# A one-layer decoder step on one core: norm factors spread by matmuls, a different start, and another queue order in the last products

## The chip, the cores and the metric

The kernel runs on one core of one Trainium2 chip. The time is the device time of one execution in microseconds (us). Five engines run their own instruction queues side by side: TensorE (PE in the rows, PEld for its weight loads), VectorE (DVE), ScalarE (ACT), GpSimd (POOL) and SyncE (SP), which issues most DMA transfers. An instruction waits at the head of its queue until what it needs is there, and all behind it wait too.

## The reference

One step over T = 576 tokens: 512 of a new sequence and 8 x 8 of running ones, model width D = 1024. All is float32.

```python
def _rmsnorm(x, g):
    y = x * lax.rsqrt(jnp.mean(x * x, axis=-1, keepdims=True) + EPS)
    return y * g

def _swiglu(h, w_up, w_down):                    # D_FF = 2816
    a, g = jnp.split(h @ w_up, 2, axis=-1)
    return (jax.nn.silu(g) * a) @ w_down

x = x + 0.5 * _swiglu(_rmsnorm(x, g_ffn1), w_ffn1_up, w_ffn1_down)
x = x + mixer(_rmsnorm(x, g_mix))                # GLA and mLSTM, 4 heads each, gated and merged
x = x + 0.5 * _swiglu(_rmsnorm(x, g_ffn2), w_ffn2_up, w_ffn2_down)
y = _rmsnorm(x, g_final)
# in the mLSTM, for t >= s:   Dm = exp(b_t - b_s + i_s - m_t), else 0;   s = (q k^T) * Dm
```

The outputs are y and the new states of both mixers.

## The kernel before, in words

Everything is stored transposed: a tile x[k] holds 128 of the 1024 channels by 576 tokens, so there are KT = 8 tiles of x, and a product accumulates over 8 channel tiles in PSUM. For accuracy each operand is split into a high and a low part (`hi` by a copy on ScalarE, `lo` = source minus `hi` on VectorE), and a product is three matmuls per channel tile and half of the tokens (HALF = 288): weight-hi by x-hi, weight-hi by x-lo, weight-lo by x-hi (`mm3`, line 121). A dense product of all channels is 8 x 3 x 2 = 48 matmuls of 288 columns (`dense`).

**Norms.** The gain is folded into the split of x (`split_x`); the factor 1/rms of a token is applied behind the product. `Norm.square` squares x[k] on ScalarE and adds the squares up on GpSimd. `Norm.start` sums them over the channels with matmuls against ones, packed in four groups of 32 partitions (`packed_sum`, line 155), then takes the root (ScalarE) and the reciprocal (VectorE, line 225). `Norm.finish` calls `unpack` (line 161): four `partition_broadcast` on GpSimd spread the packed row over all partitions into the tile r.

**The feed-forward parts (`ffn`).** Of the 22 slices f of D_FF the first two (PLAIN) are two dense products each (gate, then linear part). All others go by seven quarter-size products (a Strassen-like scheme, blocks A11, S2, A12, S3, S1, A22, S4), for which `Norm.combine` forms sums of quarters of x on VectorE and ScalarE, and `sums` forms sums of weight quarters on VectorE and GpSimd. After every group of 4 slices come 8 blocks `d` of the down product, which add into x[o]. From the third slice on the order is written by hand (`manual_schedule`): `run(i, work)` issues the matmuls of a block, then what was put off to this tick (`posts`, filled by `later(ticks, fn)`), then the block's events: weight loads (`load_up`, `load_down`), and `prep` of the block 4 ahead (`hi` on ScalarE, `lo` on VectorE). `seven` puts off the steps behind the seven products; its first one copies the result of A11 on ScalarE (tile s), and A12 adds into that same PSUM bank. When a `d` block is done, `done` adds it to x[o] on VectorE, and in the last group calls `after(o)`.

In the second feed-forward part the last 8 down products run twice, once for each half of the tokens (`parts=((0,), (1,))`), 12 matmuls each. There `after` squares x[o] for the final norm, scales x[0] and x[4] by g_final on ScalarE, and behind the third block of the second half calls `finish(ends[0])`: broadcasts, 8 products with r (k = 0 and 4 on GpSimd, the other six on VectorE) and 8 output DMAs, alternating between SP and ScalarE. The same follows for the second half at the end.

**The start.** The weights of the first two products and the 8 tiles of x are loaded; ScalarE and VectorE split them; the gate product of slice 0 runs through all 8 tiles, then the linear product, then the gate product of slice 1 (`ahead=1`), with the raw results copied out of PSUM since r is not there yet.

**Outside the hand-written order** a planner places instructions by its own cost estimates and the order of the program: the start, the first two slices, both mixers, and the final part.

**The mLSTM (`mlstm`).** For each of 4 heads GpSimd broadcasts two rows (Mb, ib, lines 963 and 964), VectorE forms Dd = min(Mb + tok, 0) in four 128x128 instructions (line 62), ScalarE takes the exponential, GpSimd multiplies by the triangular mask `tri`, and VectorE multiplies by q k^T to St; the same for the short sequences with Ds and `tri8`. Line numbers 53, 56, 62 and 65 are helpers (`tt`, `stt`, `ts`, `act`); go by the tiles.

Of the kernel before, what the change touches and what calls it, by code (L numbers as in the profile page):

```python
# [36 lines left out]
def step_kernel(ctx: ExitStack, tc: tile.TileContext, a):  # L37
# [125 lines left out]
    class Norm:  # L163
# [25 lines left out]
        def add(self, k):  # L189
            self.split(k)  # L190
            self.square(k)

        def combine(self, q, pool):
# [39 lines left out]
    def ffn(x, norm, wup, wdn, fp, after, ahead=0, parts=((0, 1),)):  # L233

# [1 line left out]

        r = early = None

        def up(f, i):
            ps = dense(wup[f, :, i], norm.parts, KT)
            if f >= ahead:
                return ps
            t = fp.tile([P, T], F32, name="raw", tag="mh3", bufs=2)
            act(halves(t), ps, AF.Copy)
            return halves(t)

        def new_mid(i):
            return [fp.tile([P, T], F32R, name=f"m{n}", tag=f"m{n}{i}", bufs=2) for n in "hl"]

        mids = [[]]
        for f in range(PLAIN):
            if f == 0 and not ahead:
                midway.append(norm.start)
            pg = early or up(f, 0)
            early = None
            if f == 0:  # L260
                for q in range(4):
                    norm.combine(q, fp)
            pa = up(f, 1)
            if f == 0:
                if ahead:
                    midway.append(norm.start)
                    early = up(1, 0)
                r = norm.finish()
# [35 lines left out]
        def prep(i):  # L304

            b = blocks[i]
            if i % 2 == 0:
                pair[0] = [wp.tile([P, KT, P], F32R, name=f"w{n}", tag=f"w{n}", bufs=3) for n in ("hi", "lo")]
            if b[0] == "d":
                n = size[b[1]]  # L310
                src = raw["d"][b[1:]]
            else:
                n = 4
                src = raw[b[0]][b[1]]
            hi, lo = (t[:, 4 * (i % 2):4 * (i % 2) + n, :] for t in pair[0])
            act(hi, src, AF.Copy)
            tt(lo, src, hi, ALU.subtract)
            parts_of[i] = hi, lo

# [37 lines left out]
        for i, b in enumerate(blocks):  # L357
            if b[0] == "d" and b[2] % 2 == 0:
                on(i - 8, load_down, i)
            on(i - 4, prep, i)  # L360

        def later(d, fn):
            posts.setdefault(tick[0] + d, []).append(fn)
# [25 lines left out]
        def run(i, work):  # L389

            for m in work:
                nc.tensor.matmul(m[0], lhsT=m[1], rhs=m[2], start=m[3], stop=m[4], skip_group_check=m[5])  # L392
            for fn in posts.pop(tick[0], ()):
                fn()
            for fn, a_ in events.pop(i, ()):
                fn(*a_)
            tick[0] += 1

        with tc.manual_schedule():
# [4 lines left out]
            for i, b in enumerate(blocks):  # L404
                if b[0] == "d":
                    _, g, o, hfs = b
                    n = size[g]
                    hi, lo = parts_of.pop(i)
                    ps = pd.tile([P, 2, 512], F32, name="pd", tag="pd")
                    work = [(ps[:, hf, :HALF], wt[:, k, :], xt[:, hf * HALF:(hf + 1) * HALF],  # L410
                             k == 0 and m == 0, k == n - 1 and m == 2, False)
                            for k in range(n) for m, (wt, xt) in enumerate(
                                ((hi, mids[g][k][0]), (hi, mids[g][k][1]), (lo, mids[g][k][0]))) for hf in hfs]
                    half = 12 if len(work) > 12 else len(work)
                    run(i, work[:half])
# [12 lines left out]
                f, n = b  # L428
# [30 lines left out]
    with pool("f1") as fp:  # L459
        x = [fp.tile([P, T], F32, name=f"x{k}") for k in range(KT)]  # L460
        n1 = Norm(x, g_ffn1, fp)

        def load(*ks):
# [4 lines left out]
        ready.append(split_w(a["wup1"][0, :, 0], KT, 2, lambda: load(0, 1)))  # L468
        load(2, 3)
        ready.append(split_w(a["wup1"][0, :, 1], KT))  # L470
        load(4, 5, 6, 7)
        nc.sync.dma_start(out=cst, in_=a["cst"])
        for k in range(KT):
            n1.square(k)
# [6 lines left out]
        ffn(x, n1, a["wup1"], a["wdn1"], fp, after, ahead=1)  # L481
        midway.append(n2.start)
        first = [win_tile(), win_tile()]
        r = n2.finish()
# [3 lines left out]
    with pool("mx") as mp:  # L488
# [416 lines left out]
        with pool("ml") as gp:  # L905
# [7 lines left out]
            def mlstm(h):  # L913
# [110 lines left out]
                ts(by16(Ds), padded(Mb), tok[:, 0, NC, h:h + 1], ALU.add, 0.0, ALU.min)  # L1024
                act(Ds, Ds, AF.Exp)
                tt(Ds, Ds, tri8, ALU.mult, eng=nc.gpsimd)
# [75 lines left out]
    with pool("f2") as fp:  # L1102
        n4 = Norm(x, None, fp)
        ends = (slice(0, HALF), slice(HALF, T))

        def finish(s):
            r = n4.finish()
            for k in range(KT):
                if k % 4 == 0:
                    tt(x[k][:, s], x[k][:, s], r, ALU.mult, eng=nc.gpsimd)  # L1110
                else:
                    stt(x[k][:, s], x[k][:, s], g_fin[:, k:k + 1], ALU.mult, r, ALU.mult)
                (nc.scalar if k % 2 else nc.sync).dma_start(out=a["yT"][:, k, s], in_=x[k][:, s])

        def after(o, part):
            n4.square(o, ends[part[0]])
            if o % 4 == 0:
                act(x[o][:, ends[part[0]]], x[o][:, ends[part[0]]], AF.Copy, scale=g_fin[:, o:o + 1])
            if part == (1,) and o == 0:
                midway.append(lambda: n4.start(ends[0]))  # L1120
            if part == (1,) and o == 2:
                finish(ends[0])

        ffn(x, n3, a["wup2"], a["wdn2"], fp, after, parts=((0,), (1,)))
        n4.start(ends[1])
        finish(ends[1])

def _lay(i):  # L1130
# [45 lines left out]
    for j in range(4):  # L1176
# [17 lines left out]
    cst = [s == t_, U, tri8, np.ones((P, P)), (np.isin(s % 32 // 8, (0, 2)) & (np.arange(NB) < 1)[None, :]),  # L1194
           s // 32 == np.arange(4)[None, :], np.full((P, 1), EPS),
           *(np.broadcast_to(s == 32 * g, (P, P)) for g in range(4))]
    out["cst"] = np.concatenate([np.asarray(v, np.float32) for v in cst], 1)
# [50 lines left out]
```

## Time and profile before

| | before |
|---|---|
| median of 3 runs | 1648.14 us (1646.6 to 1650.25) |
| the profiled execution | 1647.72 us |
| its span in the profile | 1645.9 us |
| TensorE busy | 1574.6 us, 96% |
| VectorE busy | 1092.0 us, 66% |
| ScalarE busy | 668.4 us, 41% |
| GpSimd busy | 331.7 us, 20% |
| mean granted TensorE clock | 0.989 |

The profiled execution took 1.8 us more than its span, which lies around it, and is 0.4 us below the median. A timeline row reads: start, duration, engine, line, operation, out<-in, count of merged instructions, and in brackets how long the engine had been idle and who ended that.

### The profile page before, as it was taken

What the parts mean: (1) busy time and instruction counts of PE and PEld (TensorE: products, weight loads), DVE (VectorE), ACT (ScalarE), POOL (GpSimd) and SP (SyncE); (2) the same over time, 40 slices, a digit from 0 to 9 for tenths busy, and PEclk for the clock granted to TensorE, in tenths of its full rate; (3) what the DMA queues carried; (4) which work ended last, traced back from release to release, by engine and by line L of the source; (5) the groups of instructions that cost most, each with busy time, mean ns of one, the idle gap of its engine ahead of it and who ended that gap; (6) DMA issues with size and microseconds to landing.
All of it is one profiled execution on the core that took longest, in us unless ns stands there. A gap on an engine that the chain in (4) does not pass through costs nothing.

```text
span 1645.9 us, 29867 instructions
## 1 busy us (share of the span) xinstructions
PE 1574.6 (96%) x12332; PEld 1528.1 (93%) x12332; DVE 1092.0 (66%) x1808; ACT 668.4 (41%) x1104; POOL 331.7 (20%) x333
## 2 busy tenths in 40 slices
PE   6899999999999999999999999999999999999982
PEld 5899999999989989999998989999989999999982
DVE  7797777776597667653555757633578877777752
ACT  6343333434644342531334344521454343343441
POOL 3343223221200000000111011003223422323212
PEclk9999999999999999999999999999999999999996
DMA  5232232223522313323432434442222233233231
GB/s 176 71 96 91 78 104 89 80 88 101 183 78 93 108 61 99 105 92 118 132 120 87 140 109 147 154 148 78 81 81 78 96 98 96 77 99 94 65 90 58
DMA packets 58752, 166.23 MB, mean 101 GB/s; under 512 B 6008, under 2 KB 12920, under 8 KB 57592
## 3 DMA queue, kind: packets, MB, share of 16 engines
q1 hardware_dynamic: 57464, 163.14, 30.7%
q8 instruction: 97, 1.59, 0.4%
q10 hardware_dynamic: 1152, 1.18, 0.2%
q14 instruction: 39, 0.32, 0.1%
HBM read 142.89 MB, written 21.38 MB: 100 GB/s over the span
## 4 chain that ended last, share of the span: by engine, by line
PE 85%; DVE 6%; issue 3%; ACT 3%; POOL 2%; DMA 1%; POOLq 1%; SPq 0%; ACTq 0%; DVEq 0%
PE pd L121 34%; PE pd L392 31%; PE pm L392 11%; PE pm L780 2%; DVE wlo L53 1%; PE pm L506 1%; ACT whi L65 1%; PE pm L718 1%; PE pm L1002 1%; DVE xl L56 1%; PE pm L646 1%; DVE xtl L53 1%; DVE xt L56 1%; PE pm L1055 1%; PE pm L1000 0%
## 5 line engine op out<-in xcount | busy, mean ns | idle before, releaser
L65 ACT ACTIVATE whi<-wst 128x512 fp32r<-128x512 f32 (+2 forms) x298 | 217.5, 742 | 438.5 <-PE pd L121 263.9
L53 DVE TENSOR_TENSOR wlo<-wst,whi 128x512 fp32r<-128x512 f32 (+2 forms) x298 | 267.2, 898 | 34.1 <-ACT whi L65 25.5
L121 PE MATMUL pd<-xh,whi 128*128 128x288 f32 x1168 | 259.1, 300 | 15.8 <-ACT xh L65 7.4
L121 PE MATMUL pd<-xl,whi 128*128 128x288 f32 x1168 | 254.1, 297 | 4.1 <-DVE xl L56 4.1
L121 PE MATMUL pd<-xh,wlo 128*128 128x288 f32 x1168 | 253.8, 297 | 0.8 <-DVE wlo L53 0.8
L121 PEld LDWEIGHTS pd<-xh,whi 128*128 128x128 f32 x1168 | 189.1, 189 | 22.0 <-ACT xh L65 7.4
L121 PEld LDWEIGHTS pd<-xl,whi 128*128 128x128 f32 x1168 | 188.8, 189 | 7.3 <-DVE xl L56 6.0
L121 PEld LDWEIGHTS pd<-xh,wlo 128*128 128x128 f32 x1168 | 188.7, 189 | 4.1 <-issue 3.0
L53 POOL TENSOR_TENSOR t<-t,r 128x288 f32<-128x288 f32 (+1 forms) x80 | 102.6, 1283 | 419.8 <-DVE t L53 408.1
L392 PE MATMUL pd<-mh,whi 128*128 128x288 f32 x704 | 157.3, 297 | 18.2 <-DVE x L56 18.0
L56 DVE SCALAR_TENSOR_TENSOR x<-pd,x 128x576 f32<-128x576 f32 (+1 forms) x112 | 79.6, 711 | 133.6 <-PE pd L392 107.5
L392 PE MATMUL pd<-ml,whi 128*128 128x288 f32 x704 | 156.4, 296 | 0.0
L392 PE MATMUL pd<-mh,wlo 128*128 128x288 f32 x704 | 156.2, 296 | 0.0
L392 PE MATMUL pd<-xh,whi 128*128 128x288 f32 x480 | 143.1, 298 | 5.6 <-ACT s L65 4.2
L65 ACT ACTIVATE whi<-S 128x512 fp32r<-128x512 f32 x160 | 98.9, 627 | 120.6 <-PE pd L392 69.5
L392 PE MATMUL pd<-xh,wlo 128*128 128x288 f32 x480 | 142.3, 296 | 0.0
L392 PE MATMUL pd<-xl,whi 128*128 128x288 f32 x480 | 142.1, 296 | 0.0
L392 PE MATMUL pm<-xth,wlo 128*128 128x288 f32 x480 | 141.5, 295 | 0.0
L392 PE MATMUL pm<-xtl,whi 128*128 128x288 f32 x480 | 141.5, 295 | 0.0
L392 PE MATMUL pm<-xth,whi 128*128 128x288 f32 x480 | 141.5, 295 | 0.0
L392 PEld LDWEIGHTS pd<-mh,whi 128*128 128x128 f32 x704 | 115.6, 189 | 20.4 <-issue 17.8
L53 DVE TENSOR_TENSOR wlo<-S,whi 128x512 fp32r<-128x512 f32 x160 | 131.5, 822 | 1.3 <-ACT whi L65 0.2
(307 smaller groups left out, 3244.2 us busy)
## 6 DMA issues: line engine op xcount, KB each, us to landing
wst<-in_win SPq DMA_DIRECT2D x65, 512.0 KB, 3.6
wst<-in_wup SPq DMA_DIRECT2D x47, 512.0 KB, 5.0
wst<-in_wdn SPq DMA_DIRECT2D x44, 512.0 KB, 3.6
wsu<-in_wup SPq DMA_DIRECT2D x40, 512.0 KB, 4.3
C<-in_C SPq DMA_DIRECT2D x16, 514.0 KB, 4.7
out_Cs<-C SPq DMA_DIRECT2D x16, 514.0 KB, 3.0
S<-in_S SPq DMA_DIRECT2D x4, 1024.0 KB, 5.6
out_Ss<-S SPq DMA_DIRECT2D x4, 1024.0 KB, 3.9
```

What stands on the lines that cost most here:

```text
L53: (eng or nc.vector).tensor_tensor(out=out, in0=in0, in1=in1, op=op)
L56: nc.vector.scalar_tensor_tensor(out=out, in0=in0, scalar=s, in1=in1, op0=op0, op1=op1)
L65: nc.scalar.activation(out=out, in_=in_, func=func, **kw)
L121: nc.tensor.matmul(ps[:, hf, :HALF], lhsT=wt[:, k, :], rhs=xt[:, hf * HALF:(hf + 1) * HALF], start=(k == 0 and n == 0), stop=(k == nk - 1 ...
L392: nc.tensor.matmul(m[0], lhsT=m[1], rhs=m[2], start=m[3], stop=m[4], skip_group_check=m[5])
L506: nc.tensor.matmul(out[32 * g:32 * g + 32], lhsT=src[:, o:o + 32], rhs=rhs, start=start, stop=stop)
L646: nc.tensor.transpose(out=pt[:, c, j * P:(j + 1) * P], in_=src[j][:, (c0 + c) * P:(c0 + c + 1) * P], identity=ident)
L718: nc.tensor.matmul(po[32 * g:32 * g + 32, :], lhsT=qpad(b_)[j], rhs=states(b_)[j], start=(v == 0 and j == 0), stop=False)
L780: nc.tensor.matmul(pl[:, c, :], lhsT=kk[:, cs], rhs=qq[:, cs], start=True, stop=True)
L1002: nc.tensor.matmul(po[:, c, :], lhsT=Cc[c - 1][:, d, es], rhs=qs[d][:, c * P:(c + 1) * P], start=False, stop=(d == 1))
L1055: nc.tensor.matmul(pu, lhsT=kb[:, b_ // 4, b_ % 4, j * P:(j + 1) * P], rhs=vb[:, b_ // 4, :], start=True, stop=True)
```

## The change

What it does: (1) `Norm.finish` spreads the factor by matmuls against `quarter` (rows of ones that pick one packed group), into PSUM, and copies it to r on ScalarE; with `keep=False` it stays in PSUM. (2) The start runs in `head`: the two products of slice 0 go side by side, tile of x by tile of x; squares are summed straight by matmuls (`square_sum`), without GpSimd; the weights come in three pieces each. `combine` now follows `finish`. (3) In the mLSTM the mask is a 0/-1e30 array, folded into the VectorE instruction by a minimum; GpSimd's products with the masks are gone. Its broadcasts of Mb, ib and of the head norms stay. (4) In `run`, `prep` (ScalarE's `hi`) is issued before the posts and its VectorE half (`prep_lo`) after them, and `after` comes one tick later. (5) The final norm's first half is scaled two tiles per block behind blocks 3 to 6 of the second half (four tiles on GpSimd), all its DMAs on SP; the second half reads the factor from PSUM.

```diff
+        def square_sum(self, k):
+            n = T // 4
+            if k == 0:
+                self.ps = bank([P, n], "ss")
+            sq = self.tmp.tile([P, T], F32, name="sq", tag="th"[k % 2], bufs=2)
+            act(sq, self.x[k], AF.Square)
+            def add():
+                for g in range(4):
+                    nc.tensor.matmul(self.ps[32 * g:32 * g + 32], lhsT=ones[:, :32], rhs=sq[:, g * n:g * n + n],
+                                     start=(k == 0), stop=(k == KT - 1))
+            return add
...
-        def finish(self):
+        def finish(self, keep=True):
             n = self.v.shape[1]
-            r = xs.tile([P, 4 * n], F32, name="r", tag="r", bufs=1)
-            unpack(self.v, n, r)
+            per = 2 if n == T // 4 else 4
+            r = xs.tile([P, 4 * n], F32, name="r", tag="r", bufs=1) if keep else None
+            for i in range(4 // per):
+                ps = bank([P, per * n], "rb")
+                for g in range(per):
+                    nc.tensor.matmul(ps[:, g * n:g * n + n], lhsT=quarter[:, per * i + g, :], rhs=self.v,
+                                     start=True, stop=True)
+                if not keep:
+                    return ps
+                act(r[:, i * per * n:(i + 1) * per * n], ps, AF.Copy)
             return r
...
         for f in range(PLAIN):
-            if f == 0 and not ahead:
-                midway.append(norm.start)
-            pg = early or up(f, 0)
...
+            if f == 0 and head:
+                pg, pa = head()
+                for i in range(2):
+                    ready.append(split_w(wup[1, :, i], KT))
+                norm.root()
+                r = norm.finish()
+            else:
+                if f == 0:
+                    midway.append(norm.start)
+                pg = up(f, 0)
+                pa = up(f, 1)
+                if f == 0:
+                    r = norm.finish()
             if f == 0:
                 for q in range(4):
                     norm.combine(q, fp)
...
             for m in work:
                 nc.tensor.matmul(m[0], lhsT=m[1], rhs=m[2], start=m[3], stop=m[4], skip_group_check=m[5])
+            do = events.pop(i, ())
+            for fn, a_ in do:
+                if fn is prep:
+                    fn(*a_)
             for fn in posts.pop(tick[0], ()):
                 fn()
-            for fn, a_ in events.pop(i, ()):
-                fn(*a_)
+            for fn, a_ in do:
+                if fn is not prep:
+                    fn(*a_)
...
-                            after(o, hfs)
+                            later(1, lambda: after(o, hfs))
...
+            for k in range(KT):                       # in head()
+                sums.append(n1.square_sum(k))
+                for i, k_ in ((0, k), (1, k)) if k < KT - 2 else ((k - KT + 2, KT - 2), (k - KT + 2, KT - 1)):
+                    step(i, k_)                       # 6 matmuls of product i with tile k_
+                if k >= 2:
+                    sums.pop(0)()
...
-                    ts(Dd[:, c, :], Mb[:, c * P:(c + 1) * P], tok[:, 0, c, h:h + 1], ALU.add, 0.0, ALU.min)
+                    stt(Dd[:, c, :], Mb[:, c * P:(c + 1) * P], tok[:, 0, c, h:h + 1], ALU.add, tri, ALU.min)
                 act(Dd, Dd, AF.Exp)
-                tt(Dd, Dd, tri.rearrange("p (o t) -> p o t", o=1).broadcast_to([P, NC, P]), ALU.mult, eng=nc.gpsimd)
...
+        POOLED = {0: (0, 2, 4, 6), 1: (0, 4)}
+        def finish(e, r, ks, rp=None):
+            s = ends[e]
+            for k in ks:
+                if k in POOLED[e]:
+                    tt(x[k][:, s], x[k][:, s], r if rp is None else rp, ALU.mult, eng=nc.gpsimd)
                 else:
                     stt(x[k][:, s], x[k][:, s], g_fin[:, k:k + 1], ALU.mult, r, ALU.mult)
-                (nc.scalar if k % 2 else nc.sync).dma_start(out=a["yT"][:, k, s], in_=x[k][:, s])
+                (nc.scalar if e and k % 2 else nc.sync).dma_start(out=a["yT"][:, k, s], in_=x[k][:, s])
...
+            if e and o == 2:
+                r0.append(n4.finish())
+            if e and 2 < o < 7:
+                finish(0, r0[0], (2 * o - 6, 2 * o - 5))
...
         n4.start(ends[1])
-        finish(ends[1])
+        r1 = n4.finish(keep=False)
+        rp = xs.tile([P, HALF], F32, name="rp", tag="r", bufs=1)
+        act(rp, r1, AF.Copy)
+        finish(1, r1, range(KT), rp)
```

## Rows read from the trace of the kernel before

**Rows 1.** TensorE's waits: line, waited for, total us, times, longest us.

```profile
PE pd L392 <- DVE x L56: 18.0, 9, 11.6
PE pm L1000 <- DVE St L53: 4.5, 4, 1.3
PE pd L392 <- ACT s L65: 4.2, 1, 4.2
PE pd L121 <- DVE xl L56: 4.1, 6, 0.8
PE pd L121 <- DVE t L53: 2.3, 1, 2.3
PE pd L121 <- DVE G L53: 1.7, 1, 1.7
```

**Rows 2.** The chain that ended last: start us, length us, what; two pieces.

```profile
72.72 1.60 PE pd L392 x12
...
1627.35 0.77 PE pm L155 x16
```

**Rows 3.** Timeline of TensorE in the first hand-ordered blocks.

```profile
56.82 0.61 PE L392 MATMUL pd<-xh,whi 128*128 128x288 f32 x1 [4.18 <-ACT s L65]
...
59.87 0.33 PE L392 MATMUL pm<-xth,whi 128*128 128x288 f32 x1
```

**Rows 4.** Timeline of VectorE and GpSimd in the start.

```profile
8.63 0.82 DVE L56 SCALAR_TENSOR_TENSOR xl<-x,sm,xh 128x576 fp32r<-128x576 f32 x1 [0.42 <-ACT xh L65]
...
15.85 5.47 POOL L53 TENSOR_TENSOR acc<-acc,sq 128x576 f32<-128x576 f32 x3 [0.71 <-ACT sq L65]
16.15 7.54 DVE L56 SCALAR_TENSOR_TENSOR xl<-x,sm,xh 128x576 fp32r<-128x576 f32 x4
...
48.67 1.27 POOL L53 TENSOR_TENSOR S<-wst,S 128x512 f32<-128x512 f32 x1 [7.62 <-issue]
```

**Rows 5.** ScalarE's splits of x (tile view), count, ns, first and last start.

```profile
L65 ACT ACTIVATE xh<-x,sm x8: 761/762/777, 6.6 to 15.6; 128x576 fp32r<-128x576 f32 x8
```

**Rows 6.** Busy time by stretch: us, PE, PEld, DVE, ACT, POOL, clock, DMA, GB/s.

```profile
23.60:46.30 22.70, 19.63 (x132) 18.70 (x133) 20.64 (x36) 16.20 (x24) 2.50 (x4) 0.88 0.13 36
```

**Rows 7.** Timeline in the mLSTM's first head: fp32 matmuls, mask product, wait.

```profile
816.89 1.83 PE L974 MATMUL pm<-qkm 128*128 128x128 f32 x14
...
823.49 1.27 POOL L53 TENSOR_TENSOR Dd<-Dd,cst 128x512 f32<-128x512 f32 x1 [7.54 <-issue]
...
825.54 0.71 PE L1000 MATMUL pm<-St,vtokm 128*128 128x128 f32 x4 [1.23 <-DVE St L53]
```

**Rows 8.** Timeline of ScalarE in a hand-ordered slice: the copy behind A11.

```profile
71.16 0.41 ACT L65 ACTIVATE s<-pd 128x288 f32<-128x288 f32 x1 [1.61 <-PE pd L392]
```

**Rows 9.** Timeline of one block of the last down products, all engines.

```profile
1583.30 0.45 ACT L65 ACTIVATE sq<-x 128x288 f32<-128x288 f32 x1 [1.19 <-DVE x L56]
1583.65 0.62 ACT L65 ACTIVATE whi<-wst 128x512 fp32r<-128x512 f32 x1
...
1584.30 0.88 DVE L53 TENSOR_TENSOR wlo<-wst,whi 128x512 fp32r<-128x512 f32 x1 [1.09 <-ACT whi L65]
...
1585.70 0.37 PE L392 MATMUL pd<-mh,whi 128*128 128x288 f32 x1 [0.52 <-DVE x L56]
```

**Rows 10.** Timeline of the end: first last-product matmul, stall, last matmul, final scaling.

```profile
1578.30 0.29 PE L392 MATMUL pd<-mh,whi 128*128 128x288 f32 x1
...
1620.05 0.58 PE L392 MATMUL pd<-mh,whi 128*128 128x288 f32 x1 [11.60 <-DVE x L56]
...
1626.21 0.30 PE L392 MATMUL pd<-mh,wlo 128*128 128x288 f32 x1
...
1628.49 0.60 DVE L225 RECIPROCAL v<-v 128x72 f32<-128x72 f32 x1 [1.49 <-ACT v L65]
...
1634.42 2.66 DVE L56 SCALAR_TENSOR_TENSOR x<-x,sm,r 128x288 f32<-128x288 f32 x6 [5.33 <-POOL r L161]
...
1641.58 1.54 POOL L53 TENSOR_TENSOR x<-x,r 128x288 f32<-128x288 f32 x2 [7.20 <-issue]
```

More of the change, by code (lines that the diff above doesn't have):

```diff
@@ L191, in add, with root @@
             self.square(k)
+        def square_sum(self, k):
[9 more added lines that the diff above has]
+            return add
+        def root(self):
+            self.v = v = xs.tile([P, T // 4], F32, name="v", tag="v", bufs=1)
+            act(v, self.ps, AF.Sqrt, scale=1.0 / D, bias=eps)
+            nc.vector.reciprocal(out=v, in_=v)
         def combine(self, q, pool):
@@ L225, in start, with ffn @@
             nc.vector.reciprocal(out=v, in_=v)
-        def finish(self):
+        def finish(self, keep=True):
             n = self.v.shape[1]
-            r = xs.tile([P, 4 * n], F32, name="r", tag="r", bufs=1)
-            unpack(self.v, n, r)
-            return r
-    def ffn(x, norm, wup, wdn, fp, after, ahead=0, parts=((0, 1),)):
-        r = early = None
+            per = 2 if n == T // 4 else 4
[8 more added lines that the diff above has]
+                act(r[:, i * per * n:(i + 1) * per * n], ps, AF.Copy)
+            return r
+    def ffn(x, norm, wup, wdn, fp, after, head=None, parts=((0, 1),)):
         def up(f, i):
[L244 to L249, printed above, removed]
+            return dense(wup[f, :, i], norm.parts, KT)
         def new_mid(i):
@@ L262, in ffn @@
                     norm.combine(q, fp)
[L263 to L268, printed above, removed]
             t = fp.tile([P, T], F32, name="t", tag="t", bufs=2)
@@ L360, in ffn @@
             on(i - 4, prep, i)
+            on(i - 4, prep_lo, i)
         def later(d, fn):
@@ L461, in step_kernel, with load_w @@
         n1 = Norm(x, g_ffn1, fp)
+        w0 = [[wp.tile([P, KT, P], dt, name=n, tag=n, bufs=3) for n, dt in (("wst", F32), ("whi", F32R), ("wlo", F32R))]
+              for _ in range(2)]
+        def load_w(k0, k1):
+            for i in range(2):
+                nc.sync.dma_start(out=w0[i][0][:, k0:k1, :], in_=a["wup1"][0, :, i, k0:k1, :])
+            for st, hi, lo in w0:
+                act(hi[:, k0:k1, :], st[:, k0:k1, :], AF.Copy)
+                tt(lo[:, k0:k1, :], st[:, k0:k1, :], hi[:, k0:k1, :], ALU.subtract)
         def load(*ks):
@@ L466, in load, with head, step @@
                 n1.split(k)
[L468 to L474, printed above, removed]
+        load_w(0, 2)
+        load(0, 1)
+        load_w(2, 5)
+        nc.sync.dma_start(out=ones, in_=a["cst"][:, 3 * P:4 * P])
+        load(2, 3, 4)
+        load_w(5, 8)
+        load(5, 6, 7)
+        nc.sync.dma_start(out=cst[:, :3 * P], in_=a["cst"][:, :3 * P])
+        nc.sync.dma_start(out=cst[:, 4 * P:], in_=a["cst"][:, 4 * P:])
+        def head():
+            ps = [pd.tile([P, 2, 512], F32, name="pd", tag="pd") for _ in range(2)]
+            sums = []
+            def step(i, k):
+                _, hi, lo = w0[i]
+                for n, (wt, xt) in enumerate(((hi, n1.parts[k][0]), (hi, n1.parts[k][1]), (lo, n1.parts[k][0]))):
+                    for hf in range(2):
+                        nc.tensor.matmul(ps[i][:, hf, :HALF], lhsT=wt[:, k, :], rhs=xt[:, hf * HALF:(hf + 1) * HALF],
+                                         start=(k == 0 and n == 0), stop=(k == KT - 1 and n == 2))
+            for k in range(KT):
[4 more added lines that the diff above has]
+                    sums.pop(0)()
+            raw = []
+            for p in ps:
+                t = fp.tile([P, T], F32, name="raw", tag="mh3", bufs=2)
+                act(halves(t), p[:, :, :HALF], AF.Copy)
+                raw.append(halves(t))
+            for s_ in sums:
+                s_()
+            return raw
         n2 = Norm(x, g_mix, fp)
@@ L479, in after @@
             nc.sync.dma_start(out=xd[:, o, :], in_=x[o])
-        ffn(x, n1, a["wup1"], a["wdn1"], fp, after, ahead=1)
+        ffn(x, n1, a["wup1"], a["wdn1"], fp, after, head=head)
         midway.append(n2.start)
@@ L1104, in step_kernel @@
         ends = (slice(0, HALF), slice(HALF, T))
[L1106 to L1110, printed above, removed]
+        POOLED = {0: (0, 2, 4, 6), 1: (0, 4)}
[4 more added lines that the diff above has]
+                    tt(x[k][:, s], x[k][:, s], r if rp is None else rp, ALU.mult, eng=nc.gpsimd)
                 else:
                     stt(x[k][:, s], x[k][:, s], g_fin[:, k:k + 1], ALU.mult, r, ALU.mult)
-                (nc.scalar if k % 2 else nc.sync).dma_start(out=a["yT"][:, k, s], in_=x[k][:, s])
+                (nc.scalar if e and k % 2 else nc.sync).dma_start(out=a["yT"][:, k, s], in_=x[k][:, s])
+        r0 = []
         def after(o, part):
[L1116 to L1119, printed above, removed]
+            e = part[0]
+            n4.square(o, ends[e])
+            if o in POOLED[e]:
+                act(x[o][:, ends[e]], x[o][:, ends[e]], AF.Copy, scale=g_fin[:, o:o + 1])
+            if e and o == 0:
                 midway.append(lambda: n4.start(ends[0]))
-            if part == (1,) and o == 2:
-                finish(ends[0])
+            if e and o == 2:
+                r0.append(n4.finish())
+            if e and 2 < o < 7:
+                finish(0, r0[0], (2 * o - 6, 2 * o - 5))
         ffn(x, n3, a["wup2"], a["wdn2"], fp, after, parts=((0,), (1,)))
         n4.start(ends[1])
-        finish(ends[1])
+        r1 = n4.finish(keep=False)
+        rp = xs.tile([P, HALF], F32, name="rp", tag="r", bufs=1)
+        act(rp, r1, AF.Copy)
+        finish(1, r1, range(KT), rp)
 def _lay(i):
@@ L1193, in _lay @@
     tri8 = s8 & t8 & (same8 == same8.T) & (s <= t_)
-    cst = [s == t_, U, tri8, np.ones((P, P)), (np.isin(s % 32 // 8, (0, 2)) & (np.arange(NB) < 1)[None, :]),
+    low = lambda m: np.where(m, 0.0, -BIG)
+    cst = [s == t_, low(U), low(tri8), np.ones((P, P)), (np.isin(s % 32 // 8, (0, 2)) & (np.arange(NB) < 1)[None, :]),
            s // 32 == np.arange(4)[None, :], np.full((P, 1), EPS),
```

7 lines of the change are left out of this document (4 added, 3 removed).

## The prediction

> **What bounds the kernel now.** I read the page's busy shares first: TensorE is busy almost throughout, so only its idle stretches and its slow stretches can be won. Next the waits of TensorE [rows 1]: the largest, 18.0 us, is for VectorE's `x` and lies in the last products; others sit in the start (4.2 and 4.1 us), the mLSTM (4.5), and where a norm factor is awaited (2.3 and 1.7). The chain of waits gives the unit: a dozen matmuls of 288 columns take 1.60 us, one block [rows 2]. The timelines show what stands behind each wait.
>
> In the start, VectorE's split `xl` takes 0.82 us alone, but 7.54 / 4 = 1.89 beside GpSimd's square sums of 5.47 / 3 = 1.82 [rows 4]; the last `xl` ends at 16.15 + 7.54 = 23.7, though ScalarE had split the last tile by 15.6 + 0.8 = 16.4 [rows 5]. Then VectorE is busy 20.64 of 22.70 us with the quarter sums and weight splits [rows 6]. And GpSimd's first product after a broadcast starts 7.62 us late with "issue" as the reason [rows 4]; the same 7.54 us stands in the mLSTM [rows 7], 7.20 at the end [rows 10]. ScalarE sits behind that product, and TensorE waits 4.18 us for the copy `s`, then runs a dozen in 59.87 - 56.82 = 3.05 us, the lower of the clock's two levels, 1.2 GHz [rows 3]. In the last products ScalarE and VectorE pass the ball: `sq` waits for `x`, `whi` is queued behind `sq`, `wlo` waits for `whi`, and the next `x`, for whose PSUM TensorE waits, is behind `wlo` [rows 9]. Thirteen blocks take 1620.05 - 11.60 - 1578.30 = 30.15 us, 2.32 each instead of 1.60; then come 11.60 us for broadcasts and six products put in VectorE's queue ahead of the next `x` [rows 10].
>
> **The start, taken at -16.1.** Before, the fourth hand-ordered block starts at 59.87 [rows 3], as if the first had started at 59.87 - 3 x 1.60 = 55.1 and run freely. After, TensorE can start when the first tile is split, 6.6 + 0.8 = 7.4 [rows 5]. The side-by-side products are 96 matmuls, 8 x 1.60 = 12.8. The slow level at the beginning costs 3.05 - 1.60 = 1.45 a dozen; I take 2. The 32 matmuls of the square sums: 16 of half the columns take 0.77 [rows 2], so at most 3.1; I take 2, since four at a time lie in different column groups and the 0.77 holds one drain. That gives 24.2; slice 1 adds another 12.8, the spread of r 0.6 (below): 37.6. VectorE without GpSimd's adds: 8 x 0.82 for x plus four 512-column halves of the first weights at 0.88 or less [rows 9] is 10.1 from 7.4, so 17.5, then the 20.64 us of work of [rows 6]: 38.1, or 40.2 with its present idle share. The two queues meet; I take 39.0, so 55.1 - 39.0 = 16.1. The product t x r on GpSimd now follows a factor that needs no broadcast, so the 7.62 us before it and TensorE's 4.18 go. New waits: each group of sums waits in TensorE's queue for a square, two tiles behind, with the next tile's products queued after it; ScalarE has 8 splits and 8 squares, and the squares are about as long, so 8 x (0.76 + 0.7) + weights 2.5, some 14 us from 5: they end by about 19, before the last sums are due. Bounds: 5.6 (only 4.18 + 1.45 are won) and 18. More transfers of the same bytes are issued on SP: the last tile had landed by 15.6 [rows 5] and is due after 18; that cover is some 3 us.
>
> **The spread of the factor by TensorE.** No such matmul stands in the trace. The nearest is an fp32 product of 128 columns: 14 in 1.83, 0.13 each [rows 7], so four of 144 columns cost 0.6, and two ScalarE copies of 288 columns about 0.45 each (as `sq`, [rows 9]), hidden. The factor is a wait in TensorE's in-order queue: placed right behind the sums, all products behind it would wait for root and reciprocal. At the end of the kernel these take 1629.09 - 1628.12 = 1.0 from the last sum [rows 2, 10]; with twice the columns and a table load I bound it by 2.5 per norm. Below, zero: hidden in an idle stretch. I take 0.6, as the planner has free products to put ahead. For the second norm the 1.7 us wait for G goes [rows 1] and all that follows starts earlier: 1.7 - 0.6, and 0.4 for later waits, makes -1.5 (bounds +1.5 and -3). For the third, the 2.3 us wait [rows 1] is VectorE's backlog of quarter sums, not the broadcast; `combine` now stands behind `finish` in program order, but is ready earlier: 0 (bounds +2 and -2).
>
> **The mLSTM, taken at -3.5.** Four waits of TensorE for St are 4.5 us [rows 1, 7]: Dd's mask product comes 7.54 us late on GpSimd. The mask now rides in VectorE's instruction; the new form with a second tensor costs at most some 0.1 us more, five times a head, beside TensorE's work. GpSimd's only work between broadcasts is then copies and memsets, which had no such delay after broadcasts. Late next is the chain of states on VectorE, so I take 3.5 of 4.5 (bounds 0 and 4.5 and drain, 5).
>
> **The hand-ordered blocks.** In all of them `hi` of the block four ahead goes before the posts on ScalarE, so `s` comes one `hi` (0.62, [rows 9]) later. It ended at 71.57 [rows 8] and the block that needs it started at 72.72 [rows 2]: 1.15 us of slack cover it. Cost 0. SP's weight loads keep their place among the events. `after` a tick later costs nothing before the last group, as VectorE and ScalarE wait for TensorE there.
>
> **The last products, taken at -20.8.** With `hi` ahead of `sq` the circle is cut: per block VectorE has `x` (about 0.45) and `wlo` (0.88), ScalarE `hi` (0.62) and `sq` (0.45), each under 1.60. So TensorE sets the pace. Lost now: 30.15 - 13 x 1.60 = 9.35; the stall 11.60; the last three blocks 1626.51 - 1620.05 - 4.8 = 1.66 (slow level) [rows 10]. Sum 22.6. Kept: sums of the first half 0.8, its four small spread matmuls 0.5, small waits 0.5. The reciprocal in VectorE's queue has the next `x` behind it, about 1.5 us, which the two-bank rotation of PSUM covers (a block is 1.60). The first half's scaling follows two tiles per block: on VectorE one product of 0.44 a block. Its eight DMAs move to SP, whose weight loads have all been issued by then. Bounds 13 and 22.6.
>
> Here a rule of the Trainium skill speaks against the change. What the rows show: beside a GpSimd add of 1.82 us, `xl` grew by 1.07, not by 1.82 [rows 4]. By that, VectorE's two instructions with an add and a product of GpSimd (1.54 / 2 = 0.77 each, [rows 10]) cost 0.9 + 0.9 = 1.8 a block in blocks 3 to 6: 0.8 us in all, in the small waits. The Trainium skill, page "SBUF — State Buffer", section "Who interferes with whom", says that a VectorE instruction with two SBUF inputs and a GpSimd one that reads SBUF lock each other out for a whole instruction. By that it would be 0.9 + 1.54 = 2.4 a block, 3.2 us; a rival below.
>
> **The end, taken at -10.7.** Now from the last matmul to the span's end: 1645.9 - 1626.5 = 19.4. After: add, square, sums, root and reciprocal as now, 1629.1 - 1626.5 = 2.6 [rows 10]; four small matmuls 0.5; six products on VectorE straight from PSUM 2.66 (GpSimd's two, 1.54 behind a 0.45 copy, lie beside); issue and landing as now, 1645.9 - 1643.1 = 2.8. Sum 8.6, 8.7 with hops. The broadcast and 7.20 us of GpSimd's delay go.
>
> **Sum.** 16.1 + 1.5 + 0 + 3.5 + 20.8 + 10.7 = 52.6. Span 1645.9 - 52.6 = 1593.3; the execution lies 1.8 around it: 1595.1, and 0.4 more for the median of the runs: 1595.
>
> **Rivals.**
> - VectorE's backlog keeps the start: ScalarE and VectorE alternate over the quarter sums, and the first block starts near 47. For: 91% busy [rows 6]. Against: VectorE is through with x some 6 us before 23.7 [rows 4, 5]. Gain 8 instead of 16: 1603. Chance 0.13.
> - The last products stay serial, as another circle takes over (`hi` waits for its buffer, then `x`): only 11.6 + 1.45 won there, 1603. For: 2.32 a block is double what either engine has to do; against: no wait is left that leads from `x` to `hi`. 0.08.
> - GpSimd and VectorE lock each other out in the last half: 3.2 instead of 0.8, 1598. Against: 1.07 of 1.82 [rows 4]. 0.07.
> - The planner orders the mixers anew around the changed instructions, and TensorE waits some 1 to 2.5 us more in each of 8 heads, as it did for St [rows 7]: 1603 to 1615. 0.08.
> - The change doesn't do what it says in the mLSTM: broadcasts stay, and copies behind them call the delay back: 1598. 0.04.
> - Slower: `hi` ahead of `s` in each of 40 slices. If `s` ends after the block in between, every slice loses the difference. It decides from 1.3 us a slice (40 x 1.3 = 52), that is, if `s` came 1.15 + 1.3 = 2.5 us later, four `hi` deep: 1648 and above. For: the queue is in order and `hi` may wait for a buffer or a load. Against: loads go out 11 blocks ahead, and the buffer comes free when A11 ends, where `s` starts anyway. 0.04.
> - The forecast: 0.56.
>
> **Numbers.** What can be told from no change is about 0.2%, 3.3 us. Faster by more 0.95, within 0.01, slower 0.04. Range 1586 to 1609: all bounds best or the two 1603 cases joined in part.
>
> **What would show it.** First `d` block and its predecessors: A11 of slice 2 near 39 and no wait for `s`; GpSimd's first product directly after `t`; no "issue" idle of 7 us on GpSimd in the mLSTM; last-product starts 1.6 apart and no 11.6 us wait; some 9 us from the last matmul to the end. Wrong, if the start is past 45, or the last products stay above 2 us.

## The result and the profile after

The changed kernel takes 1620.63 us (1619.18 to 1621.96, 4 runs) against 1648.78 (1646.6 to 1650.25, 4 runs): a ratio of 0.983 [0.9813, 0.9847], 28 us instead of the 53 forecast, outside the range. The profiled execution has a span of 1617.4 us.

One view cuts both spans into five stretches: the list of instructions that read the quarter sums `xth`, in each feed-forward. Its columns are min/median/max ns, then the first and the last start in us. Before:

```profile
L392 PE MATMUL pm<-xth,whi x240: 290/295/332, 50.9 to 383.1; 128*128 128x288 f32 x120
L392 PE MATMUL pm<-xth,whi x240: 292/294/298, 1240.6 to 1566.8; 128*128 128x288 f32 x120
```

and after:

```profile
L422 PE MATMUL pm<-xth,whi x240: 290/295/302, 41.5 to 378.1; 128*128 128x288 f32 x120
L422 PE MATMUL pm<-xth,whi x240: 292/295/302, 1232.9 to 1565.7; 128*128 128x288 f32 x120
```

The first hand-ordered stretch took 383.1 - 50.9 = 332.2 us and takes 336.6; the second took 326.2 and takes 332.8. The forecast cost of both was 0. The other stretches are shorter: up to the first start 41.5 for 50.9, from the last start to the end of the span 51.7 for 79.1.

What TensorE waits for, in the whole span (line, waited for: total us, times, longest; the first split of `x`, 6.7 us, stands ahead of these):

```profile
PE pd L121 <- DVE t L53: 3.6, 1, 3.6
PE pd L422 <- DVE h L53: 3.0, 4, 1.3
PE pd L422 <- ACT whi L65: 2.9, 4, 0.8
PE pd L422 <- DVE t L53: 2.6, 15, 0.4
PE pm L155 <- POOL acc L53: 2.0, 1, 2.0
PE pd L121 <- DVE G L53: 1.9, 1, 1.9
```

Of the 18.0 us for `x` of [rows 1] 0.3 are left, the 4.5 for `St` are gone, `s` is down to 1.4. New in the hand-ordered blocks are `whi` and 15 small waits for `t`; `h` is up from 1.0 to 3.0. The chain of waits says where every second slice loses time (start us, length us, what). In it `mh` and `ml` are the high and the low part of a finished slice `h`, `U` and `t` are steps behind the seven products, and `t` reads the PSUM tile `pd` that the S1 block then writes:

```profile
141.19 1.48 PE pm L422 x11
...
142.74 0.63 ACT whi L65
143.38 0.58 ACT mh L65
...
143.98 0.48 DVE ml L53
...
144.65 0.45 DVE U L53
145.10 0.06 DVE wlo L53
...
145.62 0.46 DVE t L53
...
146.12 1.85 PE pd L422 x12
```

Read upward from the last row: the S1 block takes 1.85 us, not the 1.60 of [rows 2], since `t` came late; `t` stands in VectorE's queue behind a `wlo` and `U`, these behind `ml`, and `ml` waits for `mh`. `mh` needs nothing but an `h` that is finished, yet it starts only after `whi`, and `whi` starts at 142.74 because TensorE has then ended a block. ScalarE's waits from 62 to 378 us say that this is no single case:

```profile
ACT whi L65 <- PE pd L422: 83.9, 30, 4.3
ACT whi L65 <- PE pm L422: 44.3, 27, 2.5
```

The last products run as forecast; VectorE's additions into `x` follow each other 1.57 us apart, at the pace of TensorE's blocks:

```profile
1581.11 0.46 DVE L56 SCALAR_TENSOR_TENSOR x<-pd,x 128x288 f32<-128x288 f32 x1 [0.54 <-PE pd L422]
...
1582.68 0.46 DVE L56 SCALAR_TENSOR_TENSOR x<-pd,x 128x288 f32<-128x288 f32 x1 [0.30 <-PE pd L422]
```

The end, against [rows 10] (timeline; the idle time before each is in brackets; the first row is the last matmul of the products):

```profile
1605.15 0.30 PE L422 MATMUL pd<-mh,wlo 128*128 128x288 f32 x1
...
1606.65 0.79 POOL L53 TENSOR_TENSOR acc<-acc,sq 128x288 f32<-128x288 f32 x1
...
1607.49 0.36 PE L155 MATMUL pm<-acc,cst 128*32 128x72 f32 x8 [2.04 <-POOL acc L53]
...
1609.08 1.77 PE L254 MATMUL pm<-v,cst 128*128 128x72 f32 x8 [1.10 <-DVE v L244]
1610.94 0.41 ACT L65 ACTIVATE rp<-pm 128x288 f32<-128x288 f32 x1 [2.56 <-PE pm L254]
1611.39 2.64 DVE L56 SCALAR_TENSOR_TENSOR x<-x,sm,pm 128x288 f32<-128x288 f32 x6 [2.37 <-ACT rp L65]
```

### The profile page after: what moved, and what is told of

It reads as the page before. It is cut to its first block, busy times and chain, and to the rows that moved or that the text cites. A ratio compares the mean times of both kernels' runs of the same rounds, so it can differ in the third digit from the quotient of the medians.

```text
span 1617.4 us, 29967 instructions
## 1 busy us (share of the span) xinstructions
PE 1580.9 (98%) x12420; PEld 1531.1 (95%) x12420; DVE 1078.9 (67%) x1809; ACT 667.9 (41%) x1117; POOL 310.7 (19%) x301
## 4 chain that ended last, share of the span: by engine, by line
PE 88%; DVE 6%; ACT 3%; issue 1%; POOL 1%; DMA 0%; SPq 0%; ACTq 0%; DVEq 0%; POOLq 0%
PE pd L121 36%; PE pd L422 32%; PE pm L422 10%; PE pm L855 2%; DVE wlo L53 1%; ACT whi L65 1%; PE pm L581 1%; PE pm L1062 1%; PE pm L793 1%; PE pd L532 1%; PE pm L1076 1%; DVE ml L53 1%; PE pm L721 1%; PE pm L1128 1%; DVE xt L56 0%
## 5 line engine op out<-in xcount | busy, mean ns | idle before, releaser
L65 ACT ACTIVATE whi<-wst 128x512 fp32r<-128x512 f32 (+3 forms) x301 | 217.8, 736 | 453.1 <-PE pd L121 277.8
L53 DVE TENSOR_TENSOR wlo<-wst,whi 128x512 fp32r<-128x512 f32 (+3 forms) x301 | 262.1, 872 | 23.8 <-ACT whi L65 16.2
L121 PE MATMUL pd<-xh,whi 128*128 128x288 f32 x1136 | 250.0, 297 | 5.5 <-DVE t L53 3.6
L121 PE MATMUL pd<-xh,wlo 128*128 128x288 f32 x1136 | 245.4, 294 | 0.0
L121 PE MATMUL pd<-xl,whi 128*128 128x288 f32 x1136 | 245.3, 295 | 0.0
L121 PEld LDWEIGHTS pd<-xh,whi 128*128 128x128 f32 x1136 | 182.5, 188 | 12.6 <-issue 12.2
L121 PEld LDWEIGHTS pd<-xh,wlo 128*128 128x128 f32 x1136 | 182.7, 188 | 1.4 <-issue 1.4
L121 PEld LDWEIGHTS pd<-xl,whi 128*128 128x128 f32 x1136 | 181.9, 188 | 1.2 <-issue 1.2
L422 PE MATMUL pd<-xh,whi 128*128 128x288 f32 x480 | 143.7, 299 | 7.5 <-DVE h L53 3.0
L422 PE MATMUL pd<-xl,whi 128*128 128x288 f32 x480 | 141.6, 295 | 0.0
L422 PE MATMUL pd<-xh,wlo 128*128 128x288 f32 x480 | 141.6, 295 | 0.0
L53 DVE TENSOR_TENSOR wlo<-S,whi 128x512 fp32r<-128x512 f32 x160 | 126.6, 792 | 0.8 <-ACT whi L65 0.2
```

The costliest lines, as they stand in the source:

```text
L53: (eng or nc.vector).tensor_tensor(out=out, in0=in0, in1=in1, op=op)
L65: nc.scalar.activation(out=out, in_=in_, func=func, **kw)
L121: nc.tensor.matmul(ps[:, hf, :HALF], lhsT=wt[:, k, :], rhs=xt[:, hf * HALF:(hf + 1) * HALF], start=(k == 0 and n == 0), stop=(k == nk - 1 ...
```

## The experiments

Two theories stood at first. The queue: `hi` opens a new pair of weight buffers for every second block, has to wait there for TensorE, and holds the posts behind it in ScalarE's queue; of these `mh` does the harm. The rival: the slices lose time through something else, such as the shifted start. The stretches of all profiled executions, in us, by the view above, beside the median of the runs and the ratio to the kernel before:

| kernel | to first start | first stretch | between | second stretch | to the end | median us | ratio |
|---|---|---|---|---|---|---|---|
| before | 50.9 | 332.2 | 857.5 | 326.2 | 79.1 | | |
| changed | 41.5 | 336.6 | 854.8 | 332.8 | 51.7 | 1620.6 | 0.983 |
| e1 order in the tail only | 41.5 | 329.8 | 857.5 | 326.2 | 50.5 | 1607.5 | 0.9745 |
| e2 `mh` first | 41.6 | 331.4 | 856.1 | 326.8 | 51.3 | 1607.7 | 0.9747 |
| e3 before + order | 50.8 | 338.8 | 856.4 | 332.7 | 71.8 | 1652.5 | 1.0029 |
| e4 fourth `hi` buffer | 41.6 | 329.2 | 855.6 | 325.7 | 50.0 | 1605.7 | 0.9735 |
| e5 = e4 + products on VectorE | 41.2 | 330.2 | 856.9 | 325.8 | 50.0 | 1605.3 | 0.9742 |
| e6 = e4 + early spread | 41.0 | 329.7 | 850.2 | 325.8 | 50.9 | 1599.4 | 0.9708 |
| e7 = e4 + broadcasts | 40.1 | 332.4 | 850.6 | 325.8 | 71.4 | 1621.2 | 0.9837 |
| e8 = e4 + mask product | 40.6 | 329.1 | 863.8 | 325.8 | 51.3 | 1612.4 | 0.9782 |
| e9 = e6 + start and end | 41.0 | 327.4 | 849.4 | 325.8 | 50.4 | 1595.9 | 0.9687 |

Where an edit touches nothing, "between" still differs by up to 2.7 us from profile to profile; the second stretch by 0.5.

**e1, the new order in the tail only.**

```
-                if fn is prep:
+                if fn is prep and i >= tail:
...
-                if fn is not prep:
+                if fn is not prep or i < tail:
```

> The changed kernel, but `hi` goes ahead of the posts only while the last 16 single-half blocks of the second feed-forward run; in all other hand-ordered blocks of both feed-forwards the posts come first again. Theory (the queue order costs the slices): both hand-ordered stretches get their old pace back (two slices in 35.07 us, not 35.64), the waits of TensorE for `whi`, `h` and `t` that are new in the changed kernel go, and of the 7.5 + 7.1 us lost there all comes back: 1620.6 - 14.6 = 1606 us, with the last products unchanged at about 27.5 us. Rival (the slices lost time for another reason, such as loads that meet the blocks at another time after the shorter start): two slices stay at 35.6 us and the time at 1619 to 1622 us.

Measured: 1607.48 us, ratio 0.9745 [0.9732, 0.9759]. Both stretches are at or under what they were before the change, and the last products keep their gain. The chain in the same place is TensorE alone:

```profile
139.01 1.60 PE pm L423 x12
140.61 1.60 PE pd L423 x12
```

So the order costs 336.6 - 329.8 = 6.8 and 332.8 - 326.2 = 6.6 us in the slices, as the theory has it.

**e2, `mh` ahead of `hi`.**

```
+            for fn in firsts.pop(tick[0], ()):
+                fn()
...
-            later(e[3], lambda: act(hi, h, AF.Copy))
+            firsts.setdefault(tick[0] + e[3], []).append(lambda: act(hi, h, AF.Copy))
```

> The changed kernel with its new order everywhere, but ScalarE's `mh` (the rounded copy of a finished slice) is issued ahead of `hi`; all other posts stay behind it. Theory (the harm is done through `mh`, and through `ml` and the U2 sum behind it on VectorE): ml no longer waits 1.7 us, S1 blocks go back to 1.60 us, and 8 to 14.6 us come back: 1606 to 1613 us. Rival (the harm is done through the other posts behind a waiting `hi`, the copy `s` of A11 and the Silu, or through `lo` behind the posts): 1617 to 1622 us.

Measured: 1607.74 us, 0.9747 [0.9733, 0.976]. One post out of many brings back the second stretch but for 0.6 us (326.8; e1 326.2) and most of the first (331.4; e1 329.8). Of the 1.6 us left there 1.3 are one dozen at the lower of the clock's two levels, 1.2 GHz: the granted clock from 44 to 50 us is 0.72, in e1 1.00, and the dozen takes 48.96 - 45.92 = 3.04 us, in e1 1.70:

```profile
45.92 0.61 PE L423 MATMUL pd<-xh,whi 128*128 128x288 f32 x1 [1.35 <-ACT s L65]
...
48.96 0.44 PE L423 MATMUL pm<-xth,whi 128*128 128x288 f32 x1
```

The copy `s`, which the forecast had looked at, still stands behind `hi` and is not the victim.

**e3, the kernel before with the order alone.** The edits of `run`, `prep` and `later(1, ...)` of the diff, and nothing else.

> The kernel before with one edit of the change alone: `hi` ahead of the posts, `lo` behind them, squares one block later. Theory: both hand-ordered stretches lose what they lose in the changed kernel (7.5 + 7.1 us) and the last products gain 9 to 13 us of the 20.7, since the broadcasts on GpSimd still stand in their middle: 1648.8 + 14.6 - 11 = 1652 us, 1650 to 1655. Rival (the slices lost time through the other edits): no loss in the slices, only the gain at the end: 1636 to 1640 us.

Measured: 1652.5 us, 1.0029 [1.0019, 1.004], in the forecast span. The slices lose 6.6 and 6.5 us without any other edit of the change, which ends the rival. The tail's gain was expected at 9 to 13 and is 79.1 - 71.8 = 7.3: TensorE's waits for `x` fall from 18.0 to 10.6 us, and one of 10.4, for the broadcasts, stays.

**e4, a fourth buffer for `whi`.**

```
-                pair[0] = [wp.tile(..., name=f"w{n}", tag=f"w{n}", bufs=3) for n in ("hi", "lo")]
+                pair[0] = [pl.tile(..., name=f"w{n}", tag=t_, bufs=nb) for n, pl, t_, nb in
+                           (("hi", fp, "yhi", 1) if i // 2 % 4 == 3 else ("hi", wp, "whi", 3), ("lo", wp, "wlo", 3))]
```

> The changed kernel with its order everywhere, but with a fourth buffer for the rounded weights `whi` of the feed-forwards' hand-ordered blocks, so that `hi` opens a buffer whose last reader ended two blocks earlier. Theory (a waiting `hi` is what holds the posts): ScalarE no longer waits for TensorE at `whi`, `mh` starts on time, and nearly all of the 14.6 us comes back: 1606 to 1609 us. Rival (the work of `hi` itself, 0.4 us ahead of each post, delays the posts, waiting or not): the loss stays for the most part: 1615 to 1621 us.

Measured: 1605.74 us, 0.9735 [0.9722, 0.9748], just under the expected span. The new order stands in every block here and costs nothing; ScalarE now waits for A11 at `s`, and at `whi` mostly for the sums of weights:

```profile
ACT s L65 <- PE pd L423: 68.9, 18, 4.5
ACT whi L65 <- DVE S L53: 52.4, 18, 3.6
```

Of ScalarE's waits for TensorE at `whi`, 128.2 us in 57 places in the changed kernel, 3.3 us in 4 places are left. So it was the wait of `hi` for a buffer, not its work; the waits for the sums cost the stretch nothing. The next five build on e4.

**e5, the first half's final products on VectorE.** `POOLED = {0: (), 1: (0, 4)}`.

> The kernel with the fourth hi buffer (1605.7 us), and the first half's final products all on VectorE, none on GpSimd. Theory (GpSimd's products between its additions hold back the last addition, on which the sums wait): TensorE's wait for acc falls from 2.0 to about 1.0 us, and the additions of 1.0 us that lie beside VectorE's products stay; 1 us less, 1604.7 us, to be seen in the wait rather than in the time. Rival (the additions are late by their own chain from the squares): the wait stays at 2.0 us, the time at 1605 to 1607 us.

Measured: 1605.28 us, 0.9742 [0.9728, 0.9755]: no difference that can be told. The wait for `acc` fell from 2.0 to 0.8, as it should, and a new one took its place, as VectorE's queue now holds the next `x` behind the products:

```profile
PE pd L423 <- DVE x L56: 0.9, 1, 0.9
```

**e6, the spread of the second and third norm half a product earlier.**

```
-        first = [win_tile(), win_tile()]
-        r = n2.finish()
+        first, got = [win_tile()], []
+        midway.append(lambda: got.append(n2.finish()))
+        first.append(win_tile())
+        r = got[0]
```

and the same in `ffn` for the third.

> The kernel with the fourth hi buffer (1605.7 us), and the factors of the second and third norm spread in the middle of the second product that follows the sums, not after it. Theory (these norms gave nothing because the spread matmuls, though v was ready 6 to 8 us earlier, stand behind two whole products): the waits of TensorE for G (1.9 us) and for t (3.4 us) go or shrink to under 1 us each: -3.5 to -5 us, 1601 to 1602 us. Rival (VectorE's own backlog makes G and t late, whatever the hour of the spread): both waits stay, 1605 to 1607 us.

Measured: 1599.44 us, 0.9708 [0.9694, 0.9721]: 6 us less than e4, more than expected; 5.4 of it lie in "between", 2.8 at the second norm and 2.6 at the third, each taken between rows of TensorE ahead of the norm and behind it. The wait for `G` no longer stands in the list, that for `t` is 1.9 instead of 3.4. So the two norms were late by where the planner had put the spread: in the changed kernel the second norm's `v` is ready at 421.2, its spread matmuls start at 429.2.

**e7, broadcasts again.** `Norm.finish` calls `unpack`, also at the end, where both engines read the one `r`.

> The kernel with the fourth hi buffer (1605.7 us), and every norm's factor spread by GpSimd's broadcasts again instead of TensorE's four matmuls. Theory (a broadcast next to GpSimd's additions and products costs a change of 6 to 7.5 us in the row of before, each way, and lies on the path at the start and at the end): start 3 to 8 us later, the two middle norms unchanged within 2 us, the end 7 to 12 us later: 1616 to 1626 us. Rival (the gain came from the early products and the order alone): 1604 to 1609 us.

Measured: 1621.22 us, 0.9837 [0.9822, 0.9851]: in the expected span, but by other parts. To the end of the first stretch it is 1.7 us longer (3 to 8 expected), "between" 5.0 shorter (within 2), the tail 21.4 longer (7 to 12). In the tail TensorE waits 6.9 us for `x` and 5.4 for `acc`, behind the first half's broadcast, and at the end:

```profile
1602.79 0.60 DVE L244 RECIPROCAL v<-v 128x72 f32<-128x72 f32 x1 [6.05 <-ACT v L65]
1608.14 1.10 POOL L161 PARTITION_BROADCAST r<-v  x4 [5.84 <-issue]
1609.28 2.67 DVE L56 SCALAR_TENSOR_TENSOR x<-x,sm,r 128x288 f32<-128x288 f32 x6 [5.89 <-POOL r L161]
...
1616.21 1.54 POOL L53 TENSOR_TENSOR x<-x,r 128x288 f32<-128x288 f32 x2 [6.96 <-issue]
```

A change of GpSimd between broadcast and product costs 5.84 us one way and 6.96 the other, idle with "issue" as the reason. The trace has a pair of `MODIFY_POOL_CONFIG` in GpSimd's queue ahead of each, at 1602.5 and at 1609.1 us (view of a line: count, ns, first and last start):

```profile
L161 POOLq MODIFY_POOL_CONFIG  x2: 1/1/1, 1602.5 to 1602.5; - x2
```

The Trainium skill, "GPSIMD Engine Reference", section "Instruction dispatch", has some 6 us without a visible instruction from this one to the first call of a freshly loaded kernel. The trace agrees for the broadcast, which starts 5.6 us behind the pair; the product starts 7.0 behind its pair, one more. In the middle norms the same change lies beside whole products of TensorE: the broadcasts of the second norm start 6.4 us behind its `v`, TensorE's late spread in the changed kernel 8.0.

**e8, the mask product back on GpSimd.** The three hunks of the mLSTM undone.

> The kernel with the fourth hi buffer (1605.7 us), and the masks of the matrix memory's decays multiplied on GpSimd after the exponential again, not added ahead of it on VectorE. Theory (the fold takes four waits for St of 1.1 to 1.3 us each off TensorE): they return, +4.5 to 5.3 us, 1610 to 1611 us. Rival (the 5.0 us came from the planner's other order of the same work): 1605 to 1608 us.

Measured: 1612.35 us, 0.9782 [0.9767, 0.9797]: 6.6 us more, just over the expected span. The waits are back as named, 5.1 of it. The other 1.5 can be read from the clock: behind the longest of them, 1.94 us in the first head, the granted clock drops to 0.50 (columns: us, busy us, clock, DMA share, GB/s), and TensorE falls 1.5 us further behind e4, where it stays at 1.00 there:

```profile
PE pm L1076 <- DVE St L53: 5.1, 4, 1.9
...
816.80:818.90 2.10, 2.10 (x12) 0.50 0.00 0
```

**e9, the start and the end.**

```
-            tt(t, t, r, ALU.mult, eng=nc.gpsimd)
+            tt(t, t, r, ALU.mult)
...
-            if k == 0 or k == KT - 1:
+            if k == 0 or k == KT - 1 or (s.start and k == KT - 2):
```

with e5's `POOLED`.

> The kernel with the fourth hi buffer and the early spread (1599.4 us), with three more edits: in the plain slices the product of t and r on VectorE, not on GpSimd; the first half's final products all on VectorE; and the last two squares of the second half summed by TensorE as terms of their own, so that GpSimd's last addition goes. Theory (at the start GpSimd's 2.8 us product holds the port against VectorE's h, which takes 1.83 us beside it instead of 0.75, and this chain sets the first hand-ordered blocks; at the end the last addition holds the sums): 2 to 3 us at the start, seen as the end of the fourth hand-ordered block, and 1 to 2 us between the last product and the sums: 1595 to 1597 us. Rival (VectorE has no room at the start, and the product only moves the queue): the start is the same or up to 1.5 us later, 1598 to 1601 us.

Measured: 1595.9 us, 0.9687 [0.9673, 0.9701], the fastest version here, and faster than the changed kernel. The first stretch is 2.3 us shorter than in e6, as expected; against e4, whose profile has no dozen at the lower level there (that of e6 has one, 3.05 us from 45.34 on), it is 1.8. In e6 VectorE's `h` waited for GpSimd's product, and ran beside the next work of GpSimd at more than double its 0.75 us:

```profile
35.82 2.81 POOL L53 TENSOR_TENSOR t<-t,r 128x576 f32<-128x576 f32 x1 [13.26 <-ACT t L65]
...
38.67 1.83 DVE L53 TENSOR_TENSOR h<-raw,t 128x576 f32<-128x576 f32 x1 [1.33 <-POOL t L53]
```

In e9 it runs freely, and GpSimd's sum, 1.30 us long in e6, is the one held:

```profile
36.08 5.03 POOL L53 TENSOR_TENSOR S<-wst,S 128x512 f32<-128x512 f32 x1 [11.69 <-DVE S L53]
...
37.26 0.75 DVE L53 TENSOR_TENSOR h<-raw,t 128x576 f32<-128x576 f32 x1
```

At the end the wait ahead of the sums fell from 2.06 to 0.72 us. The stretch to the end is 0.5 shorter, not 1 to 2: the new wait of e5 is there too (0.9 for `x`), and of what was won 0.87 is the clock: the four spread matmuls take 1.11 us at 1.00, in e6 1.98 at 0.50. In e4 they took 1.11 too, behind a wait of 2.0. So it is not shown that the two edits at the end are worth anything.

## Why the prediction was wrong

The changes of the profiled executions, each between the same instruction before and after:

| step | forecast | measured |
|---|---|---|
| the start (fourth block at 47.47, [rows 3]) | -16.1 | -12.4 |
| hand-ordered blocks, first and second feed-forward | 0 | +7.8, +7.1 |
| second norm | -1.5 | +1.3 |
| mLSTM | -3.5 | -5.0 |
| third norm | 0 | +0.6 |
| last products | -20.8 | -20.5 |
| the end (from the last matmul) | -10.7 | -7.4 |

They make -28.5, as the spans differ. The forecast of -52.6 was 24.1 too much; 14.9 of these are the hand-ordered blocks.

**The step that failed** is "The hand-ordered blocks": "`s` comes one `hi` ... later", "1.15 us of slack cover it. Cost 0." It counted one instruction behind `hi`, and `hi` at its own duration. A queue that is served in order passes on the wait of its head to everything behind it: where `hi` opens a buffer it waits for TensorE (57 times from 62 to 378 us, 128.2 us), and the slice's other post, `mh`, had been free to run. The trace of before could have told, for `hi` waited there too, 47 times and 88.5 us, only with the posts ahead of it:

```profile
ACT whi L65 <- PE pd L392: 56.3, 30, 3.5
...
ACT whi L65 <- PE pm L392: 32.2, 17, 3.5
```

The forecast's slower rival had the right place ("`hi` may wait for a buffer") and dismissed it because A11's end frees the buffer just when `s` may start. That holds for `s` (e2 leaves it behind `hi` and loses at most 0.6 us in the second stretch). It does not hold for `mh`, which comes two blocks into the next slice, and has `ml`, `U` and `t` behind it on VectorE. The price was far from that rival's 1.3 us a slice: 14.9 / 40 = 0.37 on average.

**The last products** were right, in size and in mechanism: the blocks run at TensorE's pace, and its waits for `x` are 0.3 us in all. VectorE's product beside GpSimd's took up to 1.02 us instead of 0.44, but of the rival in which the two lock each other out (3.2 us) nothing reached TensorE within these products; GpSimd's late additions count at the end. Of the 27.4 us of the stretch to the end, the order with the broadcasts kept is worth 7.3 (e3), the spread with the order kept 21.4 (e7).

**The end** was mis-sized by 3.3 us: 1617.4 - 1605.45 = 12.0 instead of 8.7. GpSimd's last addition held the sums, so the reciprocal ends 3.6 us after the last matmul, not 2.6; the four spread matmuls took 1.77 at a granted clock of 0.59 (1.11 at 1.00 in e4) instead of 0.5, VectorE's products start only behind ScalarE's copy `rp` (0.5), and landing is 0.6 longer.

**The start** was mis-sized by 3.7 us. A11 of slice 2 comes at 39.87, forecast 39.0. The rest of what came short lies behind it, up to the fourth block: waits of 0.92 us for `wlo` and 1.35 for `s`.

```profile
39.87 0.29 PE L422 MATMUL pd<-xh,whi 128*128 128x288 f32 x1
...
47.47 0.30 PE L422 MATMUL pm<-xth,whi 128*128 128x288 f32 x1
```

The rival "VectorE's backlog" held in this small part; e9 takes about 2 us of it by leaving GpSimd's product out. The spread took 1.0 us in TensorE's queue, not 0.6: the 14 of [rows 7] are recorded matmuls, and each fp32 product is recorded as two (the four of the spread stand as x8), so a product of 128 columns there took 0.26 us, not 0.13. The same error is in the spreads of the norms and the end.

**The norms in the middle**: the forecast hid the spread behind "free products to put ahead"; the planner put too many ahead, and the wait for `G` stayed, at 1.9 us. With the spread earlier (e6) the second norm gains 2.8 us, which makes the -1.5 of the forecast.

**The mLSTM** was right in mechanism, with no wait for `St`; taken at 3.5, it came to its bound of 5. The 6.6 us of e8 hold 1.5 of the clock besides the waits.

That e9 ends at 1595.9, where the forecast for the changed kernel lay, is chance: it needs the fourth buffer, the earlier spread and the start's product on VectorE, which the change does not have.

## What to carry over

Before an instruction is moved ahead in an engine's queue, look up what it waits for, not only how long it runs, and list every instruction that will then stand behind that wait, on this engine and on the next. A reorder that pays at one place (here 16 blocks) should be tried at that place alone; or the wait should be bought off with a buffer, which gave as much. An operation that moves to the busiest engine needs its place in that engine's order stated, or it may come late behind work that could have waited.

## What the hardware showed unexpectedly

A stop of TensorE costs more than the list of waits says. At 146.12 the list has 0.15 us (timeline of TensorE in the changed kernel):

```profile
145.68 0.29 PE L422 MATMUL pm<-xth,wlo 128*128 128x288 f32 x1
146.12 0.40 PE L422 MATMUL pd<-xth,whi 128*128 128x288 f32 x1 [0.15 <-DVE t L53]
146.36 0.30 PE L422 MATMUL pd<-xtl,whi 128*128 128x288 f32 x1
...
149.28 0.29 PE L422 MATMUL pm<-xth,wlo 128*128 128x288 f32 x1
149.48 0.37 PE L422 MATMUL pd<-xh,whi 128*128 128x288 f32 x1
149.69 0.30 PE L422 MATMUL pd<-xl,whi 128*128 128x288 f32 x1
```

In a free run starts lie 0.133 us apart. Here the first lies 0.44 behind its forerunner and the second 0.24 behind the first, 0.42 us too much; at 149.48 another 0.15 is lost that no list of waits shows. The timeline of the weight loads (PEld) shows what both places share. In the free run a load starts with the matmul before its own, 0.13 us ahead. At 146.12 load and matmul start together, and at 149.48 the load is only 0.03 us ahead:

```profile
149.15 0.19 PEld L422 LDWEIGHTS pm<-xth,wlo 128*128 128x128 f32 x1
149.45 0.19 PEld L422 LDWEIGHTS pd<-xh,whi 128*128 128x128 f32 x1
```

Two slices take 35.64 us instead of 35.07 by just these two places. The Trainium skill, "TensorE: Matmul & The Clock Gate", section "Step-by-step: what each phase is for", says that a stream of matmuls hides each one's drain, and that a single one has to pay for it; a stop of 0.15 us that costs 0.42 agrees in kind.

The four spread matmuls at the end took 1.77 us at a granted clock of 0.59 in the changed kernel (columns: us, busy us, clock, DMA share, GB/s):

```profile
1609.00:1611.00 2.00, 1.77 (x8) 0.59 0.46 148
```

and 1.11 in e4 at 1.00, behind the same wait of 2.0 us:

```profile
1594.40:1595.70 1.30, 1.11 (x8) 1.00 0.70 227
```

Which level such a short piece of work meets at the end is not settled by these runs.
